# Two decay-matrix buffers, a third gated-output buffer, a later group norm and weight low parts summed by DMA in a Mamba-2 mixer

## The chip, the core and the metric

The kernel runs on one core of a Trainium2 chip. The metric is the device time of one execution in microseconds; the numbers given are the median of the runs and their extremes. A change of 0.3% is about what a measurement of this kernel can tell from none.

## What is computed

One inference step of a two-layer decoder trunk, 576 tokens of width 1024 (512 of a prompt, and 8 sequences of 8 sampled tokens), everything in float32. Layer 0 is a SwiGLU FFN at half weight, a Mamba-2 mixer (SSD) and a second FFN; layer 1 the same with a pooling mixer; then a final norm. Only the SSD is touched. Cut to what matters, it is:

```python
proj = h @ w_in
z, xbc, dt_raw = jnp.split(proj, [D_INNER, D_INNER + CONV_DIM], axis=-1)
xbc, conv_new = causal_dwconv(xbc, conv0, conv_w, conv_b)
xs, Bm, Cm = jnp.split(silu(xbc), ...)          # 32 heads of 64, 8 groups, state 128
dt = softplus(dt_raw + dt_bias);  A = -exp(a_log)
# ssd_scan, in chunks of 128 tokens:
a_cum = cumsum(dt * A)
decay = exp(where(tril, a_cum[l] - a_cum[s], -inf))
y_diag = einsum('bclsgr,bcsgrp->bclgrp', cb[..., None] * decay, x * dt)
y_off  = einsum('bclgn,bclgr,bcgrpn->bclgrp', C, exp(a_cum), h_starts)
y = (y_diag + y_off + d_skip * xs) * silu(z)
y = y * rsqrt(mean over the group's 256 channels of y*y + EPS) * norm_g
return y @ w_out, ssm_new, conv_new
```

## The kernel before

*Matmuls.* Activations lie transposed, channels on the partitions, 576 tokens along the free dimension in two halves of 288. A float32 product is made of three products of rounded parts: weight high by activation high, high by low, low by high. `load` fetches a weight tile of 128 columns (512 KB of the input weight, 256 KB of the output weight) into the pool `raw`, which has two buffers. `block` (L311) makes the parts of up to four 128x128 pieces of it in one `wb` tile, of which the ring has six: ScalarE (ACT) rounds the piece to the high part (L317), and GpSimd (POOL) or VectorE (DVE) subtracts it from the piece for the low part (L318). In the SSD `proj` and `outproj` name POOL for it; the FFNs and the pooling mixer use DVE and POOL as well and stay as they are. `mm` (L334) then issues 24 matmuls for a block of four pieces, 48 for an input projection.

*The SSD.* Of its 48 input projections for z, x, B and C, the two for the first B and C tile take weights that were prepared earlier (`wconv`); 46 go through `proj`. A group loop (L966 to 1003) runs over 8 groups of 4 heads. A group's B and C tiles have been projected and convolved by `conv_in` (L632) during the group before; its two x tiles are projected at its head. `gsum` (L935) squares and sums the two gated outputs of the *previous* group, `rnat` (L184) sums them over the channels on TensorE (PE), and `rstd` (L187 to L198) makes the reciprocal root by two Newton steps on DVE, ten small operations. `gnorm` (L950) lets PE spread the result over all partitions (`rbcast`, L218), multiplies the outputs by it (L955) and splits them into high and low parts `yn`, which `outproj` (L900) multiplies by the output weight in groups 2, 4, 6 and after the loop.

*A pair of heads* (`pair`, L781). The decay matrix `m` (128 x 2 x 576) starts as a broadcast load of the cumulated step sizes `ad` from device memory, issued by SyncE (SP). POOL masks it (L834 to 836), ACT takes the exponential (L839), DVE multiplies it by C times B (L840, L841). Before it is used PE transposes the x tile (L797) and the old states `nat` (L800), DVE copies the latter to `h0t` (L813), and PE multiplies them by C (L822). At the end PE multiplies `m` by the weighted x (L870, L872: the diagonal part `py`). `m` has a single buffer (L787), so that the load for the next pair starts when L872 of this pair is done. The gated output is `yt` (two buffers, L978), the gate `zs` (two buffers, L960).

*The start.* The step sizes go through a chain of small DVE operations (L709 to L745, a softplus by series, a cumulated sum, decay factors), to memory and back, and through transposes on PE (L749 on) into the tables `decp`, `dskp`, `anat`, `wsn` that each pair reads.

*Order.* The engines run their instructions in order. A scheduler puts the written program into one order per engine; the sections `pin` keep some of PE's instructions as written. Two accumulators in PSUM take turns in the SSD: a projection cannot start until DVE has read the one before the last (L638 to 640 for a conv).

Of the kernel before, what the change touches and what calls it, by code (L numbers as in the profile page):

```python
# [8 lines left out]
F32 = mybir.dt.float32  # L9
F32R = mybir.dt.float32r  # L10
I32 = mybir.dt.int32
AF = mybir.ActivationFunctionType
ALU = mybir.AluOpType
# [4 lines left out]
P = 128  # L18
# [3 lines left out]
NB = 8  # L22
NS = 8
T = SEQ + NB * NS
# [25 lines left out]
def trunk(ctx, tc, x_prompt, x_sample, state_ssm, state_conv, state_pool,  # L50
# [26 lines left out]
    def misc():  # L77
        return psum["misc"].tile([P, 512], F32, name="misc")
# [232 lines left out]
    def block(src, eng=None, pool=None):  # L311
        w = (pool or spl).tile([P, 2, 4, P], F32R, name="wb")
        k = src.shape[1]
        hi, lo = w[:, 0, 0:k], w[:, 1, 0:k]
        if src.ndim == 4:
            hi, lo = [a.rearrange("p k (c f) -> p k c f", c=src.shape[2]) for a in (hi, lo)]
        S.copy(out=hi, in_=src)  # L317
        (eng or V).tensor_tensor(out=lo, in0=src, in1=hi.bitcast(F32), op=ALU.subtract)  # L318
        return w

    def load(src, shape):
# [6 lines left out]
    def unit(src, eng=None):  # L328
        kn = src.shape[1]
        v = load(src, src.shape[1:])  # L330
        bl = [block(v[:, k:min(k + 4, kn)], eng) for k in range(0, kn, 4)]
        return [(bl[k // 4][:, 0, k % 4], bl[k // 4][:, 1, k % 4]) for k in range(kn)]

    def mm(pt, w, acts):  # L334
        n, kn = 0, len(acts)
        for (wh, wl), (ah, al) in zip(w, acts):
            for lt, a in ((wh, ah), (wh, al), (wl, ah)):
                for h in range(2):
                    PE.matmul(out=pt[:, h, 0:HALF], lhsT=lt, rhs=a[:, h * HALF:(h + 1) * HALF],  # L339
                              start=n == 0, stop=n == 3 * kn - 1)  # L340
                n += 1
# [246 lines left out]
    def ssd(tail):  # L588
# [5 lines left out]
        with ExitStack() as st:  # L594
# [31 lines left out]

            def proj(c0, w=None):
                pt = acc_tile()
                mm(pt, w or unit(win[:, :, c0:c0 + P], G), hs)
                return pt  # L630

            def conv_in(ct):  # L632
# [111 lines left out]
                ps = slice(32 * r, 32 * r + 32)  # L744
                V.tensor_tensor(out=rhs[ps, :, 4 * r:4 * r + 4], in0=e[ps, P + NS - 1:LW:NS].unsqueeze(1).broadcast_to([32, 16, 4]), in1=bc(mh[ps], 4), op=ALU.mult)  # L745
            V.tensor_scalar(out=mh[0:32], in0=mh[0:32], scalar1=hv[0:32, 2:3], scalar2=None, op0=ALU.mult)
            pt = misc()
            self_ = sel.rearrange("h a b -> h (a b)")
            PE.matmul(out=pt[:, 0:P], lhsT=self_, rhs=rhs.rearrange("h a b -> h (a b)"), start=True, stop=True)  # L749
            PE.matmul(out=pt[:, P:P + 16], lhsT=self_[0:32], rhs=mh[0:32], start=True, stop=True)  # L750
            V.tensor_copy(out=decp, in_=pt[:, 0:P].rearrange("p (a b) -> p a b", b=NB))
            V.tensor_copy(out=dskp, in_=pt[:, P:P + 16])

            pt, pt2 = misc(), misc()
            for i, src in enumerate((ac, q, wd)):
                PE.transpose(out=pt[:, i * P:(i + 1) * P], in_=src[:, 0:P], identity=ident)
                for r in range(2):
                    ps = slice(32 * r, 32 * r + 32)
                    PE.matmul(out=pt2[ps, i * HEADS:(i + 1) * HEADS], lhsT=src[0:64, P:LW], rhs=ident[0:64, ps], start=True, stop=True)
            w3 = dp.tile([64, 3, 32], F32, name="w3")  # L760
            V.tensor_copy(out=w3, in_=wd[0:64, P:LW].unsqueeze(1).broadcast_to([64, 3, 32]))
            for r in range(2):
                ps = slice(32 * r, 32 * r + 32)
                PE.matmul(out=pt2[0:96, P + r * HEADS:P + (r + 1) * HEADS], lhsT=w3.rearrange("h a s -> h (a s)"), rhs=ident[0:64, ps], start=True, stop=True)
            V.tensor_copy(out=wsn, in_=pt2[0:96, P:P + 64].rearrange("s (q h) -> s q h", q=2))
            V.tensor_copy(out=anat[:, 0:4], in_=pt[:, 0:384].rearrange("p (i c h) -> p c i h", i=3, c=4))
            V.tensor_copy(out=anat[0:64, 4], in_=pt2[0:64, 0:96].rearrange("p (i h) -> p i h", i=3))
            V.tensor_scalar(out=anat[:, 0:4, 0], in0=anat[:, 0:4, 0], scalar1=-1.0, scalar2=None, op0=ALU.mult)
            V.tensor_scalar(out=anat[0:64, 4, 0], in0=anat[0:64, 4, 0], scalar1=-1.0, scalar2=None, op0=ALU.mult)

            pin = tc.keep_in_program_order

# [8 lines left out]
            def pair(g, j, bt, ctl, bnat, bblk, cbs, xst, yt):  # L781
# [2 lines left out]
                nat = wk.tile([P, NB, P], F32, name="nat")  # L784
                sv = state_ssm[0, :, h0:h0 + 2].rearrange("b h p n -> (h p) b n")
                nc.sync.dma_start(out=nat, in_=sv)
                m = wk.tile([P, 2, T], F32, name="m", bufs=1)  # L787
                nc.sync.dma_start(out=m, in_=ad[h0:h0 + 2].unsqueeze(0).broadcast_to([P, 2, T]))
                eb = wk.tile([P, T - P], F32, name="eb", bufs=1)
                for h2 in range(2):  # L790
# [109 lines left out]
            def outproj(k0, kn, ds):  # L900
                for d in ds:
                    pd = acc_tile()
                    mm(pd, unit(wout[:, k0:k0 + kn, d * P:(d + 1) * P], G), [yn[k0 + k] for k in range(kn)])
                    add_x(d, pd, 1.0, False)

            def silu(ct, dst):
# [50 lines left out]

            def zproj(k):
                pz = proj(k * P)
                zs = wk.tile([P, T], F32, name="zs")  # L960
                V.tensor_tensor(out=halves(zs), in0=pz[:, :, 0:HALF], in1=rb2, op=ALU.mult)
                S.activation(out=zs, in_=zs, func=AF.Silu)
                return zs

            ys = None
            for g in range(8):  # L966
                bt = gp.tile([P, T], F32, name="bt")
                ctl = gp.tile([P, T], F32, name="ctl")
                silu(16 + g, bt)
                silu(24 + g, ctl)  # L970
                if g == 7:
                    conv_state(2)
                    conv_state(3)
                args = (bt, ctl) + group(bt, ctl)
                xs, nys = [], []

                def run(j):
                    yt = wk.tile([P, T], F32, name="yt")  # L978
                    if g % 2 == 0 and g:
                        outproj(max(2 * g - 6, 0), 4 if g > 2 else 2, range(4 * j, 4 * j + 4))  # L980
                    pair(g, j, *args, xs[j], yt)
                    nys.append(yt)
                    if j == 0 and g < 7:
                        for ct in (17 + g, 25 + g):
                            pre[ct] = conv_in(ct)

                for j in range(2):
                    xst = wk.tile([P, T], F32, name="xst")
                    pre[2 * g + j] = conv_in(2 * g + j)
                    silu(2 * g + j, xst)  # L990
                    if 2 * g + j in (9, 15):
                        conv_state(g // 6)
                    xs.append(xst)
                    if g and j == 0:
                        r = gsum(ys)
                    if g and j == (g < 7):
                        gnorm(g - 1, ys, r)
                    if g == 7:
                        run(j)
                if g < 7:  # L1000
                    run(0)
                    run(1)
                ys = nys
            gtile(7)
# [203 lines left out]
```

## Time and profile before

| | us |
|---|---|
| median of 3 runs | 2381.2 (2376.72 to 2383.12) |
| the profiled execution | 2382.37, its span 2380.6 |
| mean granted clock of PE | 0.978 |

The profile shows one execution, the profiled one, with span times counted from its start. The SSD stage lies from about 417 to 1017 us. In the rows quoted below, a line like `m<-ad` names the tile written and the one read; `x16` is a count of instructions; the granted clock is a share of 2.4 GHz. A wait is put down to the instruction that ended it.

### The profile page before, as it was taken

To read this page: it belongs to the slowest core of one execution; us is meant where nothing else is said; L and a number is where in the kernel's file an instruction comes from. 1 tells how busy PE (TensorE), PEld (TensorE's weight loads), DVE (VectorE), ACT (ScalarE), POOL (GpSimd) and SP (SyncE) were. 2 spreads that over 40 slices of the span, in tenths; PEclk is the share of its full clock that TensorE was granted. 3 is DMA by queue.
4 is the path that set the end of the run, shared out by engine and by line. 5 is a ranking of instruction groups with operands and counts; after the bars stand their busy time and mean duration, and the time that the engine had idled before them with its cause. 6 is when DMAs were issued, how large, how long until landed. Compare 5 with 4: busy or idle time off the path is not lost.

```text
span 2380.6 us, 43792 instructions
## 1 busy us (share of the span) xinstructions
PE 2295.6 (96%) x17572; PEld 2258.1 (95%) x17572; DVE 1888.3 (79%) x2950; ACT 1055.3 (44%) x1949; POOL 1020.2 (43%) x796
## 2 busy tenths in 40 slices
PE   8999999999899899989999999999999999999998
PEld 7999999898899899889999999999999899999997
DVE  8987777678787786799777799788776859778876
ACT  6444435444455445454443355344444344434433
POOL 4555440334334343354545444455531325555530
PEclk9999999999999999999999999999999999999999
DMA  5223222242434334322322322222321242313221
GB/s 148 89 89 107 89 81 65 72 138 83 127 96 121 114 116 127 112 80 72 107 89 89 98 89 81 83 79 88 107 81 58 65 118 89 107 63 98 89 72 58
DMA packets 272903, 222.23 MB, mean 93 GB/s; under 512 B 8321, under 2 KB 269041, under 8 KB 272700
## 3 DMA queue, kind: packets, MB, share of 16 engines
q1 hardware_dynamic: 269172, 218.04, 30.0%
q8 instruction: 139, 2.28, 0.4%
q10 hardware_dynamic: 3528, 1.39, 0.2%
q14 instruction: 64, 0.52, 0.1%
HBM read 206.46 MB, written 12.94 MB: 92 GB/s over the span
## 4 chain that ended last, share of the span: by engine, by line
PE 73%; DVE 17%; DMA 4%; ACT 3%; issue 2%; POOL 0%; SPq 0%; ACTq 0%; DVEq 0%; POOLq 0%
PE acc L370 34%; PE acc L433 21%; PE acc L339 12%; DMA m<-ad 3%; DVE wb L318 3%; DVE cacc L648 2%; DVE wh L256 1%; ACT m L839 1%; PE acc L480 1%; DMA raw<-in_ffn_w_up 1%; DVE ws L1090 1%; PE misc L870 1%; PE misc L826 1%; DVE wh L267 1%; ACT L839 1%
## 5 line engine op out<-in xcount | busy, mean ns | idle before, releaser
L370 PE MATMUL acc<-wh,wb 128*128 128x288 f32 x6888 | 922.1, 295 | 3.2 <-DVE wb L318 1.3
L370 PEld LDWEIGHTS acc<-wh,wb 128*128 128x128 f32 x6888 | 917.6, 189 | 5.0 <-DVE wb L318 2.0
L433 PE MATMUL acc<-ghi,wb 128*128 128x288 f32 x2752 | 482.2, 296 | 0.5 <-DVE x L411 0.5
L317 ACT CAST wb<-raw 128x512 fp32r<-128x512 f32 (+1 forms) x440 | 265.0, 607 | 364.7 <-PE acc L339 155.4
L433 PEld LDWEIGHTS acc<-ghi,wb 128*128 128x128 f32 x2752 | 406.0, 189 | 1.2 <-DVE x L411 1.2
L318 POOL TENSOR_TENSOR wb<-raw,wb 128x512 fp32r<-128x512 f32 (+1 forms) x154 | 207.7, 1351 | 312.1 <-ACT wb L317 294.4
L339 PE MATMUL acc<-hhi,wb 128*128 128x288 f32 x1824 | 336.9, 302 | 0.9 <-DVE m L1065 0.8
L318 DVE TENSOR_TENSOR wb<-ws,wb 128x512 fp32r<-128x512 f32 x328 | 326.6, 1007 | 13.3 <-ACT wb L317 13.2
L318 DVE TENSOR_TENSOR wb<-raw,wb 128x512 fp32r<-128x512 f32 (+1 forms) x286 | 274.4, 975 | 63.5 <-ACT wb L317 63.4
L317 ACT CAST wb<-ws 128x512 fp32r<-128x512 f32 x328 | 202.2, 621 | 233.2 <-PE acc L370 216.8
L433 PE MATMUL acc<-glo,wb 128*128 128x288 f32 x1376 | 294.3, 296 | 0.0
L339 PEld LDWEIGHTS acc<-hhi,wb 128*128 128x128 f32 x1824 | 276.3, 193 | 3.5 <-DVE m L1065 1.1
L411 DVE SCALAR_TENSOR_TENSOR x<-acc,x 128x576 f32<-128x576 f32 x160 | 120.5, 753 | 191.2 <-PE acc L433 190.9
L351 POOL TENSOR_TENSOR ws<-raw,ws 128x512 f32<-128x512 f32 x82 | 154.8, 1887 | 247.9 <-DVE wb L318 241.9
L318 POOL TENSOR_TENSOR wb<-rd,wb 128x512 fp32r<-128x512 f32 x128 | 175.3, 1379 | 183.1 <-ACT wb L317 182.9
L317 ACT CAST wb<-rd 128x512 fp32r<-128x512 f32 x196 | 114.2, 593 | 247.6 <-PE acc L433 212.9
L433 PEld LDWEIGHTS acc<-glo,wb 128*128 128x128 f32 x1376 | 221.4, 189 | 0.0
L339 PE MATMUL acc<-hlo,wb 128*128 128x288 f32 x912 | 201.9, 301 | 0.0
L350 POOL TENSOR_TENSOR ws<-raw 128x512 f32<-128x512 f32 x82 | 123.9, 1511 | 176.3 <-DVE wb L318 176.3
L348 POOL TENSOR_TENSOR ws<-raw 128x512 f32<-128x512 f32 x82 | 125.0, 1525 | 76.7 <-DMA raw<-in_ffn_w_gate 68.9
L339 PEld LDWEIGHTS acc<-hlo,wb 128*128 128x128 f32 x912 | 150.2, 193 | 0.4
L349 POOL TENSOR_TENSOR ws<-ws,raw 128x512 f32<-128x512 f32 x82 | 131.9, 1608 | 8.4 <-DVE wb L318 1.5
(329 smaller groups left out, 2902.8 us busy)
## 6 DMA issues: line engine op xcount, KB each, us to landing
raw<-in_ffn_w_gate SPq DMA_DIRECT2D x41, 1024.0 KB
raw<-in_ffn_w_up SPq DMA_DIRECT2D x41, 1024.0 KB
rd<-in_ffn_w_down SPq DMA_DIRECT2D x80, 512.0 KB
raw<-in_ssd_w_in SPq DMA_DIRECT2D x48, 512.0 KB
m<-ad SPq DMA_DIRECT2D x16, 576.0 KB
nat<-in_state_ssm SPq DMA_DIRECT2D x16, 512.0 KB
out<-nat SPq DMA_DIRECT2D x16, 512.0 KB
raw<-in_ssd_w_out SPq DMA_DIRECT2D x24, 256.0 KB
```

Source lines behind the costliest of these rows:

```text
L317: S.copy(out=hi, in_=src)
L318: (eng or V).tensor_tensor(out=lo, in0=src, in1=hi.bitcast(F32), op=ALU.subtract)
L339: PE.matmul(out=pt[:, h, 0:HALF], lhsT=lt, rhs=a[:, h * HALF:(h + 1) * HALF], start=n == 0, stop=n == 3 * kn - 1)
L348: G.tensor_tensor(out=s[0], in0=blk[2], in1=blk[3], op=ALU.add)
L349: G.tensor_tensor(out=s[1], in0=s[0], in1=blk[0], op=ALU.subtract)
L350: G.tensor_tensor(out=s[2], in0=blk[2], in1=blk[0], op=ALU.subtract)
L351: G.tensor_tensor(out=s[3], in0=blk[1], in1=s[1], op=ALU.subtract)
L370: PE.matmul(out=pt[:, m, 0:HALF], lhsT=wb[:, j, k], rhs=hh[k, h][:, slot], start=n == 0, stop=n == 11)
L411: V.scalar_tensor_tensor(out=halves(x[:, d]), in0=pt[:, :, 0:HALF], scalar=scale, in1=halves(x[:, d]), op0=ALU.mult, op1=ALU.add)
L433: PE.matmul(out=pd[:, q, 0:HALF], lhsT=lt, rhs=a[:, q * HALF:(q + 1) * HALF], start=n == 0, stop=n == 3 * kn - 1)
L648: V.scalar_tensor_tensor(out=a[:, 0:n], in0=ext[:, k:k + n], scalar=cw[:, k * 32 + ct:k * 32 + ct + 1], in1=a[:, 0:n], op0=ALU.mult, op1=A ...
L839: S.activation(out=m[0:n, h2, t0:t0 + n], in_=m[0:n, h2, t0:t0 + n], func=AF.Exp, bias=anat[0:n, c, 0, h0 + h2:h0 + h2 + 1])
```

## The change

It has five parts, all in the SSD.

1. `m` has two buffers (the pool's own number) in place of one.
2. `yt` has three in place of two, `zs` one in place of two.
3. `gnorm` of the previous group is called after the first pair of a group (`run(0)`), where it was called after the projection of the group's second x tile and so ahead of that pair (in the last group after the first x tile).
4. The transposes and copies of the step sizes are put into a function `spread`, called in the first group just ahead of its first pair.
5. In `proj` and `outproj` the low part is not subtracted on POOL: ACT writes the negated high part, and a DMA that POOL issues adds the piece from `raw` to it in place. 124 subtractions of POOL become 124 passes of ACT and 124 such DMAs (116 of 256 KB, 8 of 128 KB); 92 of them belong to the 46 projections, 32 to the output tiles.

```diff
@@ block
         S.copy(out=hi, in_=src)
-        (eng or V).tensor_tensor(out=lo, in0=src, in1=hi.bitcast(F32), op=ALU.subtract)
+        if eng == "dma":
+            S.activation(out=lo, in_=hi.bitcast(F32), func=AF.Identity, scale=-1.0)
+            G.dma_start(out=lo.bitcast(F32), in_=src, accum_op=ALU.add)
+        else:
+            (eng or V).tensor_tensor(out=lo, in0=src, in1=hi.bitcast(F32), op=ALU.subtract)
@@ proj
-                mm(pt, w or unit(win[:, :, c0:c0 + P], G), hs)
+                mm(pt, w or unit(win[:, :, c0:c0 + P], "dma"), hs)
@@ ssd, after the step sizes
-            pt = misc()
-            self_ = sel.rearrange("h a b -> h (a b)")
-            PE.matmul(out=pt[:, 0:P], lhsT=self_, rhs=rhs.rearrange("h a b -> h (a b)"), start=True, stop=True)
...
+            def spread():
+                pt = misc()
+                self_ = sel.rearrange("h a b -> h (a b)")
+                PE.matmul(out=pt[:, 0:P], lhsT=self_, rhs=rhs.rearrange("h a b -> h (a b)"), start=True, stop=True)
...
@@ pair
-                m = wk.tile([P, 2, T], F32, name="m", bufs=1)
+                m = wk.tile([P, 2, T], F32, name="m")
@@ outproj
-                    mm(pd, unit(wout[:, k0:k0 + kn, d * P:(d + 1) * P], G), [yn[k0 + k] for k in range(kn)])
+                    mm(pd, unit(wout[:, k0:k0 + kn, d * P:(d + 1) * P], "dma"), [yn[k0 + k] for k in range(kn)])
@@ zproj
-                zs = wk.tile([P, T], F32, name="zs")
+                zs = wk.tile([P, T], F32, name="zs", bufs=1)
@@ run
-                    yt = wk.tile([P, T], F32, name="yt")
+                    yt = wk.tile([P, T], F32, name="yt", bufs=3)
@@ group loop
                     if g and j == 0:
                         r = gsum(ys)
-                    if g and j == (g < 7):
-                        gnorm(g - 1, ys, r)
                     if g == 7:
                         run(j)
+                        if j == 0:
+                            gnorm(g - 1, ys, r)
                 if g < 7:
+                    if g == 0:
+                        spread()
                     run(0)
+                    if g:
+                        gnorm(g - 1, ys, r)
                     run(1)
                 ys = nys
```

Up to the SSD and after its end the order on PE is the same in both programs. The places that matter are in the SSD; group 5 stands for the others here. The lines of the changed kernel are four or five higher.

PE, before, around the broadcast of the norm of group 4 (`rr`, L218), which is written in group 5 (`acc` is a projection, `s` and `xst` are the first transposes of the pair):

```order
L339 MATMUL acc_9499<-hhi,wb 128x288 x4
L339 MATMUL acc_9499<-hlo,wb 128x288 x2
L218 MATMUL misc<-ident,rr 128x128 x4
L218 MATMUL misc<-ident,rr 128x64
L777 MATMUL misc<-ident,s_9321 96x128 x2
L797 MATMUL misc<-ident,xst 128x128 x4
L797 MATMUL misc<-ident,xst 64x128
```

PE, changed, at the same broadcast:

```order
L866 MATMUL misc<-ident,ht 128x128
L868 MATMUL misc<-ctl,ht 128x128 x3
L870 MATMUL misc<-ident,ch 128x128 x2
L875 MATMUL misc<-m,xdt 64x128 x8
L877 MATMUL misc<-m,xd_4653 64x64 x2
L343 MATMUL acc_9637<-hlo,wb 128x288
L343 MATMUL acc_9637<-hhi,wb 128x288 x4
L343 MATMUL acc_9637<-hlo,wb 128x288 x2
L343 MATMUL acc_9637<-hhi,wb 128x288 x4
L343 MATMUL acc_9637<-hlo,wb 128x288 x2
L343 MATMUL acc_9637<-hhi,wb 128x288 x2
L218 MATMUL misc<-ident,rr 128x128 x4
```

The broadcast stood ahead of the group's first pair; now it stands behind that pair's last matmuls with `m`.

DVE, before, at `rstd` of the same norm (`m` is the matrix of the group's first pair, `rm` the first operation of `rstd`):

```order
L643 COPY tails<-ext 128x24
L840 TENSOR_TENSOR m<-m,cbs 128x2x512
L928 TENSOR_TENSOR bsp<-bns,bsp 32x256
L841 TENSOR_TENSOR m<-m,cbs 64x2x64
L189 TENSOR_SCALAR rm<-misc 128x5
L190 TENSOR_SCALAR rr<-rm 128x5
L192 TENSOR_TENSOR rt<-rr 128x5
L648 SCALAR_TENSOR_TENSOR cacc<-ext,cw,cacc 128x600
```

DVE, changed:

```order
L647 COPY tails<-ext 128x24
L845 TENSOR_TENSOR m<-m,cbs 128x2x512
L846 TENSOR_TENSOR m<-m,cbs 64x2x64
L652 SCALAR_TENSOR_TENSOR cacc<-ext,cw,cacc 128x600 x2
L845 TENSOR_TENSOR m<-m,cbs 128x2x512
L933 TENSOR_TENSOR bsp<-bns,bsp 32x256
L652 SCALAR_TENSOR_TENSOR cacc<-ext,cw,cacc 128x600
L189 TENSOR_SCALAR rm<-misc 128x5
L846 TENSOR_TENSOR m<-m,cbs 64x2x64
```

The multiply of the matrix of the group's second pair has come forward as well: both pairs' L845 now stand ahead of `rstd`, and also ahead of the copies to `h0t` (L818), which follow `rstd`.

POOL, before, in group 5 (the mask of `m`, the subtractions, and `bblk`, which the state update needs):

```order
L834 AFFINE_SELECT m<-m 128x2x512
L835 AFFINE_SELECT m<-m 64x2x64
L836 AFFINE_SELECT m<-m 64x2x64
L318 TENSOR_TENSOR wb<-raw,wb 128x512
L930 TENSOR_TENSOR bblk<-bsp,bmask 96x512 x2
L318 TENSOR_TENSOR wb<-raw,wb 128x512
L636 MEMSET ext 128x3
L318 TENSOR_TENSOR wb<-raw,wb 128x512 x4
```

POOL, changed:

```order
L839 AFFINE_SELECT m<-m 128x2x512
L840 AFFINE_SELECT m<-m 64x2x64
L320 DMA wb<-raw 128x512
L841 AFFINE_SELECT m<-m 64x2x64
L935 TENSOR_TENSOR bblk<-bsp,bmask 96x512 x2
L320 DMA wb<-raw 128x512
L640 MEMSET ext 128x3
L320 DMA wb<-raw 128x512 x2
```

An issue of a DMA now stands where a subtraction stood, also behind the masks that wait for the load of `m`.

## Rows read from the trace of the kernel before

**Rows 1.** Page, part 1: busy time by engine, share of the span, instructions.

```profile
PE 2295.6 (96%) x17572; PEld 2258.1 (95%) x17572; DVE 1888.3 (79%) x2950; ACT 1055.3 (44%) x1949; POOL 1020.2 (43%) x796
```

**Rows 2.** Windows: first FFN, whole SSD stage, and four of its stalls.

```profile
core 0: us, PE busy (x) PEld busy (x) DVE busy (x) ACT busy (x) POOL busy (x), PEclk, DMA share, GB/s
120.00:360.00 240.00, 240.00 (x1811) 240.00 (x1810) 185.49 (x228) 96.11 (x157) 120.13 (x79) 1.00 0.29 91
417.00:1017.00 600.00, 560.63 (x4615) 537.96 (x4615) 462.62 (x1018) 289.48 (x618) 225.93 (x232) 0.96 0.38 111
471.40:486.20 14.80, 9.68 (x49) 8.39 (x49) 8.00 (x20) 5.18 (x11) 4.29 (x5) 0.65 0.32 86
610.40:622.70 12.30, 4.18 (x18) 4.19 (x18) 11.64 (x23) 5.68 (x11) 7.66 (x7) 0.58 0.15 43
817.10:827.50 10.40, 3.74 (x17) 3.24 (x17) 9.05 (x20) 3.80 (x8) 4.58 (x5) 0.67 0.35 98
958.40:964.00 5.60, 3.20 (x15) 2.70 (x15) 4.79 (x15) 3.00 (x6) 1.51 (x2) 0.70 0.21 61
```

**Rows 3.** Waits of PE in the SSD stage: us in total, times, longest.

```profile
PE misc L218 <- DVE rr L197: 20.4, 6, 6.7
PE acc L339 <- DVE ext L640: 8.1, 1, 8.1
PE misc L749 <- DVE rhs L745: 4.7, 1, 4.7
PE acc L339 <- DVE x L409: 2.4, 2, 2.0
PE misc L184 <- DVE sqacc L941: 1.2, 1, 1.2
```

**Rows 4.** Chain of waits, 797 to 826 us (group 5): start us, us, what.

```profile
799.23 0.12 PE misc L872 x4
...
800.51 8.20 DMA m<-ad
...
814.69 1.27 DVE m L841
...
816.07 1.83 DVE rr L190
...
817.93 1.18 DVE rt L192
...
823.77 1.41 PE misc L218 x5
```

**Rows 5.** Chain of waits, 596 to 622 us (group 2).

```profile
598.22 6.76 DMA m<-ad
...
609.27 1.22 DVE m L840
```

**Rows 6.** Chain of waits, 440 to 480 us (start of the SSD).

```profile
450.09 1.25 DVE nat L709
...
460.80 0.25 DVE nat L716
...
462.15 1.25 DVE nat L716
...
468.65 1.31 DVE nat L718
```

**Rows 7.** Instructions of line 648: ns min/median/max, first and last start.

```profile
L648 DVE SCALAR_TENSOR_TENSOR cacc<-ext,cw,cacc x96: 823/844/2646, 439.8 to 973.0; 128x600 f32<-128x600 f32 x96
```

**Rows 8.** Groups by line, SSD stage: busy us, mean ns, idle before and releaser.

```profile
L318 POOL TENSOR_TENSOR wb<-raw,wb 128x512 fp32r<-128x512 f32 (+1 forms) x126 | 171.7, 1365 | 235.7 <-ACT wb L317 218.2 <-ACT tails L642 8.7 <-issue 8.6
...
L317 ACT CAST wb<-raw 128x512 fp32r<-128x512 f32 (+1 forms) x130 | 77.6, 602 | 126.9 <-PE acc L339 116.0 <-DMA raw<-in_ssd_w_out 5.9 <-issue 2.1
```

**Rows 9.** DMA queues, SSD stage: packets, MB, share of 16 engines.

```profile
q1 hardware_dynamic: 104305, 64.28, 37.0%
```

**Rows 10.** Chain of waits, 1005 to 1020 us (256 KB load of an output weight).

```profile
1012.69 4.33 DMA rd<-in_ssd_w_out
```

More of the change, by code (lines that the diff above doesn't have):

```diff
@@ L746, in ssd @@
             V.tensor_scalar(out=mh[0:32], in0=mh[0:32], scalar1=hv[0:32, 2:3], scalar2=None, op0=ALU.mult)
-            pt = misc()
-            self_ = sel.rearrange("h a b -> h (a b)")
-            PE.matmul(out=pt[:, 0:P], lhsT=self_, rhs=rhs.rearrange("h a b -> h (a b)"), start=True, stop=True)
-            PE.matmul(out=pt[:, P:P + 16], lhsT=self_[0:32], rhs=mh[0:32], start=True, stop=True)
-            V.tensor_copy(out=decp, in_=pt[:, 0:P].rearrange("p (a b) -> p a b", b=NB))
-            V.tensor_copy(out=dskp, in_=pt[:, P:P + 16])
@@ L754, in ssd @@
-            pt, pt2 = misc(), misc()
-            for i, src in enumerate((ac, q, wd)):
-                PE.transpose(out=pt[:, i * P:(i + 1) * P], in_=src[:, 0:P], identity=ident)
+            def spread():
+                pt = misc()
+                self_ = sel.rearrange("h a b -> h (a b)")
+                PE.matmul(out=pt[:, 0:P], lhsT=self_, rhs=rhs.rearrange("h a b -> h (a b)"), start=True, stop=True)
+                PE.matmul(out=pt[:, P:P + 16], lhsT=self_[0:32], rhs=mh[0:32], start=True, stop=True)
+                V.tensor_copy(out=decp, in_=pt[:, 0:P].rearrange("p (a b) -> p a b", b=NB))
+                V.tensor_copy(out=dskp, in_=pt[:, P:P + 16])
+                pt, pt2 = misc(), misc()
+                for i, src in enumerate((ac, q, wd)):
+                    PE.transpose(out=pt[:, i * P:(i + 1) * P], in_=src[:, 0:P], identity=ident)
+                    for r in range(2):
+                        ps = slice(32 * r, 32 * r + 32)
+                        PE.matmul(out=pt2[ps, i * HEADS:(i + 1) * HEADS], lhsT=src[0:64, P:LW], rhs=ident[0:64, ps], start=True, stop=True)
+                w3 = dp.tile([64, 3, 32], F32, name="w3")
+                V.tensor_copy(out=w3, in_=wd[0:64, P:LW].unsqueeze(1).broadcast_to([64, 3, 32]))
@@ L757, in ssd @@
                 for r in range(2):
                     ps = slice(32 * r, 32 * r + 32)
[L759 to L769, printed above, removed]
+                    PE.matmul(out=pt2[0:96, P + r * HEADS:P + (r + 1) * HEADS], lhsT=w3.rearrange("h a s -> h (a s)"), rhs=ident[0:64, ps], start=True, stop=True)
@@ new lines, in spread @@
+                V.tensor_copy(out=wsn, in_=pt2[0:96, P:P + 64].rearrange("s (q h) -> s q h", q=2))
+                V.tensor_copy(out=anat[:, 0:4], in_=pt[:, 0:384].rearrange("p (i c h) -> p c i h", i=3, c=4))
+                V.tensor_copy(out=anat[0:64, 4], in_=pt2[0:64, 0:96].rearrange("p (i h) -> p i h", i=3))
+                V.tensor_scalar(out=anat[:, 0:4, 0], in0=anat[:, 0:4, 0], scalar1=-1.0, scalar2=None, op0=ALU.mult)
+                V.tensor_scalar(out=anat[0:64, 4, 0], in0=anat[0:64, 4, 0], scalar1=-1.0, scalar2=None, op0=ALU.mult)
```

## The prediction

> **What bounds the kernel now.** I read the page first. TensorE (PE) is busy for 96% of the span [rows 1], so the time can only come out of the 4% in which it is not, and out of stretches in which its granted clock is low. The table of windows says where they lie: a stretch inside the first FFN has PE busy for all of its 240 us at a clock of 1.00, with 1811 matmuls, that is 0.133 us for one; the SSD stage has it busy for 560.6 of 600 us at a clock of 0.96 [rows 2]. So 39.4 us are idle there. A mean of 0.96 means 0.04 x 600 x 2 = 48 us at the lower of the two levels, 1.2 GHz instead of 2.4, in part while PE was idle anyway: at most 24 us of work lost. The other stages keep their instructions and their order.
>
> The list of PE's waits in the SSD tells what ends the idle time [rows 3]. 20.4 us are six waits of the broadcast of a group's norm factors (L218) for the last step of `rstd` (L197). 8.1 us are one wait for an accumulator that the conv's copy (L640) had not emptied. 4.7 us are the one wait for the step sizes (L745) at the start. PE waits nowhere for a weight's low part (L318); none such is in the list.
>
> The chain of waits shows why `rstd` is late [rows 4]. The diagonal matmuls of one pair end at 799.35 us; only then is the single `m` buffer free. The load that follows lands 8.2 us after 800.51, mask and exponentials follow, and the second multiply of `m` starts on VectorE (DVE) at 814.69, the first some 1.7 us before it. DVE works in order, and `rstd` stands right behind that multiply: 1.83 and 1.18 us for two of its operations, then seven more among other work, and L218 starts at 823.77. PE had reached it 6.66 us before. In the group that waited for L640 it is the same chain: load at 598.22, multiply at 609.27 [rows 5], then `rstd`, then L640.
>
> After a wait PE works at the low level for a while. The window from 817.1 has 0.67: 0.33 x 10.4 x 2 = 6.9 us at half clock, of which PE worked in the last 3.7, so 1.9 us are lost; by the same working the window from 958.4 loses 1.6, the one from 610.4 loses 2.1 and the one from 471.4 loses 4.9 [rows 2].
>
> **The change, part by part.** *Norm broadcast behind the pair.* L218 moves behind the next pair's diagonal matmuls. Counting the instructions in the new order at the durations of the trace, PE now has 26 to 65 us of work between the last use of the buffer and L218, where it had 14 to 20. DVE needs, from that last use, 11.5 us to the first late multiply (10 to 13.6 in the groups read; 11.05 from the load's start in [rows 5], 13.6 in [rows 4]) and 5 to 9.1 us of its own work to the end of `rstd`: 23 us at the worst, under 26. So all six waits go: 20.4 us, and 6 x 1.75 = 10.5 of clock.
>
> *The accumulator wait.* The output projections of that group now come behind the pair as well, and three accumulations lie between the accumulator and its next use. Gone: 8.1 + 2.1 = 10.2.
>
> *Second `m` buffer.* By itself it shortens no work. It lets the first pair of each group have its matrix early. But on DVE the *second* pair's multiply, whose load still starts when the previous pair is finished, stands ahead of `rstd` and of the copies of the first pair's state (`h0t`), for which PE's matmuls at L822 (L827 now) wait. PE's work from the buffer's release to those matmuls is 16 to 47 us, DVE's need 11.5 + 5.3 to 11. In the groups 1 and 2 alone it is short: 17.3 against 17.7 and 16.3 against 16.8; with 13.6 for the 11.5 both wait 2.6 us. I take 2 us for each, nearer the upper end, since the load that I can follow through all its steps [rows 4] is the one of 13.6, and 1.7 of clock: 7.4 given back. The ends are 0 and 8.6.
>
> *Third `yt`, one `zs`.* The third buffer is what lets the norm come a pair later; it costs nothing. `zs` is written by one projection and read by one multiply, before the next pair's projection; nothing, as long as that multiply isn't held for a whole pair (6.4 us of matmuls for a projection, 48 x 0.133).
>
> *Step sizes later.* Some eight matmuls and their copies stand behind more projection work. More important there is the contention: on the chain from 440 us the DVE operations of the softplus take 1.25 to 1.40 us, five times, where another of the same line (L716) takes 0.25 [rows 6]. They run beside the subtractions on GpSimd (POOL), which go. The conv's multiply-add shows the same thing over the stage, 0.82 us at the least and 2.65 at the most [rows 7]. Five times 1.05 is 5.2 us, as much as the 5.1 that PE is idle at this place (14.80 less 9.68 in the window from 471.4 [rows 2]). With the clock's 4.9 there are 10 to be had; I take 7, since ACT becomes busier in the same stretch.
>
> *Smaller waits* (L409, L184; 3.6 us): they are DVE's lateness too; I take 2.
>
> *Low parts by DMA.* Of the window's 126 subtractions of 1.37 us, 172 us together, all but a few leave POOL and in all 124 negations, priced like the cast's 0.60, come to ACT (75 us on 289 of 600) [rows 2, 8]. Neither is the bound. What is new is the landing time L of a 256 KB accumulate, of which the trace has none. From below: the transfers of the stage took 37.0% of 600 us for 64.28 MB [rows 9], so 0.26 MB take 0.9 us, or 1.8 if the destination is read too. From above: the longest landing of `m`, 8.2 us for 576 KB [rows 4]. I take 4.3, that of a 256 KB weight tile [rows 10], the nearest in size.
>
> Two things must hold. A low part must be there before PE wants it: six blocks in the ring give five blocks of 24 matmuls, 16 us, against 0.6 + 0.6 + 1.3 (POOL's issue, bounded by nothing and the subtraction that it replaces) + 4.3 = 6.8; with L = 8.2 it is 10.7. And the two `raw` buffers must turn round in time, since a tile is held until its accumulates have landed. For the 46 projection tiles: load 6.0 (6.76 us for 576 KB in rows 5, scaled to 512), four ACT passes 2.4, issue 1.3, L: 9.7 + L. For the 32 output tiles 4.3 + 1.2 + 1.3 + L = 6.8 + L. The mean is 8.5 + L; two buffers and 78 tiles in 600 us allow 15.4. The stage then takes 78 x (8.5 + L) / 2 us: up to L = 5.8 that is under the 557 of the forecast, at 6.9 it is 600 and all of the gain is gone, and beyond that the kernel is slower. At 4.3 it costs nothing.
>
> Here the Trainium skill speaks against this part. "SBUF — State Buffer", "Who interferes with whom": descriptors of a DMA issued by GpSimd are written through a port that VectorE holds for the whole of an instruction in certain fast modes, copies among them; and "DMA: Bandwidth & Descriptors", "Anatomy of one DMA", gives about 2.0 us plus bytes over 436 GB/s, 2.6 us for this transfer by my estimate. By the second the loop would have 1.7 us more room than I give it; by the first each issue could be held for as long as one DVE instruction. No trace here shows either; the sum stays as it is.
>
> Worked from rows, a hold of an issue by one DVE operation costs up to 1.2 us (the multiply of 609.27 [rows 5]): L = 5.5, still under 5.8, but only just.
>
> **The sum.** 20.4 + 10.5 + 10.2 + 7 + 2 = 50 less 7.4 gives 42.7. The profiled execution took 2382.4 us (1.2 above the median of 2381.2, so the two stand for the same time): **2340 us**. All idle time and 18 us of clock would be 57: 2325; with the whole 24, 2319.
>
> **Rivals.** *1. The waits only move.* The late multiply still stands ahead on DVE; if the load of `m` lands later than now, among the accumulates' traffic (0.38 DMA share [rows 2], some 32 MB more on 64), every group waits at L827, 2 to 4 us plus clock, and the first group loses its 7. For it: the load takes up to 8.2 us already. Against: by the same count PE's margin is 2 to 24 us in the groups 3 to 7. Five more groups at 2 us each are 10 us less gain, at 4.7 and 1.7 of clock 32: 2350 to 2372.
>
> *2. No change.* The turn-round of `raw` takes the place of the norm's waits: an L between 6.7 and 7.1 eats the gain to within 7 us of 2382. For it: ACT's casts and POOL's issues stand in order behind exponentials and masks that wait for `m`. Against: the 4.33 of a tile of this size.
>
> *3. Slower.* The same loop with L over 7.1: with 8.2 the mean tile takes 16.7 us, 78 tiles on two buffers 651, so 51 us more than now, 2433; the sign hangs on 2.8 us of a time that no row shows. For it: an accumulate reads what it writes; and the issue can be held.
>
> Something about 0.3%, 7 us, is what a measurement of this kernel can tell from no change. The forecast, 2325 to 2350, has 0.63; rival 1 0.16; rival 2 0.08; rival 3 0.13. So faster 0.79, the same 0.08, slower 0.13. The range takes in the forecast, rival 1 and the edge of rival 2, with the 2319 of the fullest gain at its lower end: 2320 to 2376.
>
> **What would show it.** Right: L218 gone from PE's list of waits, the SSD's stretch of 600 us some 43 shorter at a clock of 0.98 or more, the conv's multiply-add near 0.84 us at its longest, waits of 2 us at L827 in two early groups, no wait of PE on a weight block. Wrong: a wait of PE at L343 on a DMA into `wb`, waits of SP's queue for `raw` that end with an accumulate, landings of over 6 us for it, or waits at L827 in all groups.

## The result and the profile after

The changed kernel takes 2404.85 us (median of 4 runs, 2401.27 to 2407.57) where the kernel before takes 2381.39 in the same runs: the ratio is 1.0101, with an interval of 1.0079 to 1.0122. It is slower by 1%; the forecast was 2340. The profiled execution has a span of 2405.8 us, 25.2 more than before.

The window of the whole SSD stage, from the first transposes of the convolution's state to the last output tile, shows where the time went. The first row below is the kernel before, the second the changed one (columns as in [rows 2]).

```profile
428.50:1015.70 587.20, 547.83 (x4506) 525.55 (x4505) 457.60 (x998) 286.82 (x614) 221.96 (x221) 0.96 0.39 111
```

```profile
428.40:1041.40 613.00, 558.19 (x4505) 533.06 (x4504) 401.68 (x1000) 355.28 (x741) 165.00 (x221) 0.95 0.68 159
```

The stage is 25.8 us longer, all of the difference. PE's idle time in it rose from 39.4 (587.20 less 547.83) to 54.8 us; the time at the lower clock rose from 47.8 to 58.0 us, of which PE worked in 37.8 and 51.3, so that it costs 6.7 us more. That leaves 3.7 us of the 25.8, in PE's busy time, which no row explains. DVE is busy for 56 us less, although it runs as many instructions (998 and 1000), POOL for 57 less, ACT for 68 more, and the DMA engines are busy for 0.68 of the stage where it was 0.39. The page has a queue that was not there before, and the landing time that no row of before could show:

```profile
q0 software_dynamic: 17856, 31.47, 7.8%
...
wb<-raw POOLq DMA_DIRECT2D x116, 256.0 KB, 4.0
```

An accumulate of 256 KB lands 4.0 us after its issue, in the median; the forecast had taken 4.3. Its 31.47 MB take 7.8% of sixteen engines' span, 5.96 us of one such share per MB (0.078 x 2405.8 / 31.47), where the 218 MB of the loads and stores take 3.3.

PE's waits in the stage (us in total, times, longest) answer to [rows 3]:

```profile
PE acc L343 <- DVE x L413: 10.6, 6, 3.6
PE misc L782 <- ACT s L780: 6.3, 1, 6.3
PE misc L827 <- ACT h0t L815: 6.2, 3, 3.6
PE misc L866 <- DVE ht L861: 5.6, 2, 3.4
PE misc L805 <- DVE rm L189: 4.7, 2, 3.3
PE misc L782 <- ACT fin L890: 4.4, 2, 2.2
```

The wait at L218 is gone altogether, and of the 8.1 for the conv's copy 3.8 are left. In their place PE waits in other places for ACT and DVE. The first row had 2.4 us before (L409 in [rows 3]) and the fourth 1.0; the other four were not in the list. None is a wait for a weight block. SP's waits from 417 to 1040 us tell what is behind them, first of the changed kernel, then of the one before:

```profile
SPq L329 <- DMA wb<-raw: 381.9, 74, 16.0
```

```profile
SPq L325 <- POOL wb L318: 287.6, 59, 12.8
```

SP stands for 382 us at the next weight load, waiting for an accumulate to land. Before, SP's wait cost PE nothing, as the weight was there when ACT wanted it; now ACT waits for it. Of ACT's waits, the first row is its wait for a free weight block, that is for PE (116.0 before [rows 8]); the others are for raw tiles, 93 us together, where the kernel before has 5.9 for output tiles [rows 8] and 1.1 for projection tiles (last row):

```profile
ACT wb L317 <- PE acc L343: 63.9, 37, 4.1
ACT wb L317 <- DMA raw<-in_ssd_w_out: 53.2, 18, 6.5
ACT wb L317 <- DMA raw<-in_ssd_w_in: 39.9, 15, 6.6
```

```profile
ACT wb L317 <- DMA raw<-in_ssd_w_in: 1.1, 1, 1.1
```

ACT works in order, so a cast that waits for its raw tile also holds the copies behind it that PE wants. Of PE's four waits of 2 us or more for ACT's `h0t` and `fin`, three come right behind such a cast (at 513, 723 and 873 us), the fourth behind the exponentials of `m`.

The chain of waits from 554 us shows how this reaches `m` (start us, us, what):

```profile
558.94 2.29 DMA raw<-in_ssd_w_out
...
561.25 0.04 POOLq L320
...
562.59 5.20 DMA wb<-raw
...
567.85 0.37 SPq L329
...
568.33 4.29 DMA m<-ad
...
572.69 1.28 ACT L844
```

An accumulate lands; only then can SP issue the next load of a raw tile; and the load of `m` stands behind that on SP's queue. The buffer of this `m` had been free since 563.1, when the last matmuls with the matrix that was in it had ended. Over the pairs 2 to 15 the load of `m` is issued more than 1 us after its buffer is free in eight, by 1.1 to 5.4 us, and from issue to mask it takes 7.4 us in the mean, where it took 6.2 before.

### The profile page after: what moved, and what is told of

Its sections match the earlier page's. It is cut to its first block, busy times and chain, and to the rows that moved or that the text cites. A ratio compares the mean times of both kernels' runs of the same rounds, so it can differ in the third digit from the quotient of the medians.

```text
span 2405.8 us, 44158 instructions
## 1 busy us (share of the span) xinstructions
PE 2304.3 (96%) x17572; PEld 2264.2 (94%) x17572; DVE 1822.1 (76%) x2950; ACT 1122.6 (47%) x2075; POOL 958.6 (40%) x796
## 3 DMA queue, kind: packets, MB, share of 16 engines
q0 software_dynamic: 17856, 31.47, 7.8%
q10 hardware_dynamic: 3528, 1.39, 0.2%
## 4 chain that ended last, share of the span: by engine, by line
PE 68%; DVE 14%; DMA 9%; issue 4%; ACT 4%; POOL 1%; SPq 0%; POOLq 0%; DVEq 0%; ACTq 0%
PE acc L374 34%; PE acc L437 21%; PE acc L343 9%; DMA wb<-raw 3%; DVE wb L322 3%; DMA m<-ad 3%; DVE wh L256 1%; DMA raw<-in_ssd_w_in 1%; DMA raw<-in_ssd_w_out 1%; ACT m L844 1%; PE acc L484 1%; ACT wb L317 1%; DVE cacc L652 1%; DVE ws L1099 1%; DVE wh L267 1%
## 5 line engine op out<-in xcount | busy, mean ns | idle before, releaser
L322 DVE TENSOR_TENSOR wb<-raw,wb 128x512 fp32r<-128x512 f32 (+1 forms) x286 | 265.3, 942 | 72.5 <-ACT wb L317 72.3
L320 POOL DMA_DIRECT2D wb<-raw x124 | 107.7, 875 | 319.9 <-ACT wb L319 202.2
```

The costliest lines, as they stand in the source:

```text
L320: G.dma_start(out=lo.bitcast(F32), in_=src, accum_op=ALU.add)
```

## The experiments

The SSD of every kernel here is put in order anew by the scheduler, so each edit moves more than the part it names. Two edits that remove nothing PE waited for at length (e12, and m on ACT's queue in e14) cost 7 to 9 us. A difference of that size between two kernels, e1's gain of 9 us among them, is therefore no proof of a cause by itself; where one is named below, a row of waits shows it. Ratios are to the kernel before on the same chip.

| kernel | what it is | us | ratio (interval) |
|---|---|---|---|
| after | the change | 2404.85 | 1.0101 (1.0079 to 1.0122) |
| e1 | change without the DMA part | 2373.42 | 0.997 (0.9954 to 0.9987) |
| e2 | DMA part alone | 2425.41 | 1.0182 (1.0165 to 1.0199) |
| e3 | change, 3 raw, 4 wb | 2382.86 | 1.0001 (0.9991 to 1.0011) |
| e4 | change, 4 wb | 2401.27 | 1.0086 (1.0063 to 1.011) |
| e5 | change, raw in 4 halves | 2390.58 | 1.0039 (1.0024 to 1.0054) |
| e6 | e5 without DMA part | 2371.65 | 0.9964 (0.995 to 0.9977) |
| e7 | change, m on ACT's queue | 2401.6 | 1.0082 (1.0065 to 1.0099) |
| e8 | change, DMA for output tiles alone | 2381.23 | 1.0005 (0.9995 to 1.0014) |
| e9 | e5 and m on ACT's queue | 2354.98 | 0.9879 (0.9852 to 0.9906) |
| e10 | e5, negation on DVE | 2379.93 | 0.9992 (0.9978 to 1.0007) |
| e11 | e1 with the early norm | 2382.06 | 0.9996 (0.9986 to 1.0006) |
| e12 | e1, `tails` copied by ACT | 2382.67 | 0.9999 (0.9987 to 1.0011) |
| e13 | e9 without DMA part | 2380.04 | 0.9994 (0.9984 to 1.0004) |
| e14 | e1 and m on ACT's queue | 2379.99 | 0.999 (0.9979 to 1.0002) |

**e1: the reordering alone.** Against the changed kernel:

```diff
-                mm(pt, w or unit(win[:, :, c0:c0 + P], "dma"), hs)
+                mm(pt, w or unit(win[:, :, c0:c0 + P], G), hs)
...
-                    mm(pd, unit(wout[:, k0:k0 + kn, d * P:(d + 1) * P], "dma"), [yn[k0 + k] for k in range(kn)])
+                    mm(pd, unit(wout[:, k0:k0 + kn, d * P:(d + 1) * P], G), [yn[k0 + k] for k in range(kn)])
```

> The change without its fifth part: the low parts in the SSD are subtracted on POOL as before, the other four parts stay. Theory A (the two raw buffers, now held until an accumulate has landed, pace the SSD): 2340 us (2325 to 2355), as the forecast's sum without the DMA part; L218 gone from PE's waits, SP's waits for raw end with a subtraction again. Rival B (the new order is what costs: norm behind the pair, both multiplies of m ahead of rstd): 2390 us or more, with PE's waits at L782, L805 and L827 as in the changed kernel. Rival C (m's load stands behind raw loads on SP's queue and lands later in the accumulates' traffic): like A here, 2340 to 2355.

It takes 2373.42 us: faster than before by 0.3%, and 31 under the changed kernel. So the DMA part is what made the change slower, and rival B falls; but theory A's 2340 falls with it, since the rest gains 9 us, not 40. PE's waits of e1 (417 to 1007 us) show why:

```profile
PE acc L343 <- DVE x L413: 8.5, 6, 3.3
PE misc L754 <- DVE rhs L749: 3.9, 1, 3.9
PE misc L827 <- DVE h0t L818: 3.4, 4, 1.5
PE acc L343 <- DVE ext L644: 2.9, 1, 2.9
PE misc L866 <- DVE ht L861: 2.7, 1, 2.7
PE misc L802 <- DVE rm L189: 2.4, 1, 2.4
```

L218 is gone as forecast. The waits that stand here are for DVE in other places. In the chain from 562 us DVE works off the norm (L960), the split (L409) and the copies of the next pair (L814) one after the other while PE waits for the conv's copy (L642 to L644) to free its accumulator:

```profile
562.54 1.70 DVE yt L960 x4
...
564.80 0.76 DVE yn L409
...
566.22 1.56 DVE yn L409
567.79 0.60 DVE xw L814
...
569.51 0.36 DVE ext L642
...
570.45 1.62 PE acc L343 x7
```

The norm put behind the first pair falls into the stretch in which DVE has to close one pair and open the next. And DVE is slow beside POOL's products and subtractions, which read two tiles each: one copy of 128x24 took 3.45 us while POOL ran its two `bblk` products and two subtractions (first row DVE, the others POOL):

```profile
721.70 3.45 DVE L647 COPY tails<-ext 128x24 f32<-128x24 f32 x1
```

```profile
719.65 3.02 POOL L935 TENSOR_TENSOR bblk<-bsp,bmask 96x512 fp32r<-96x512 f32 x2 [2.02 <-DVE bsp L933]
722.64 2.48 POOL L322 TENSOR_TENSOR wb<-raw,wb 128x512 fp32r<-128x512 f32 x2
```

**e2: the DMA part alone**, the same two calls and the branch in `block` put into the kernel before.

```diff
+        if eng == "dma":
+            S.activation(out=lo, in_=hi.bitcast(F32), func=AF.Identity, scale=-1.0)
+            G.dma_start(out=lo.bitcast(F32), in_=src, accum_op=ALU.add)
```

> The kernel before with the fifth part alone: low parts by negation and accumulating DMA. Theory A: 2400 to 2440 us, slower than the kernel before by 20 or more, since the raw loop now takes 15.3 us a tile (mean of the changed kernel's 74 full cycles) and the norm's waits are all still there. Rival B: 2375 to 2390, the DMA part alone changes nothing. Rival C: 2390 to 2410, the late m makes each of the six norm waits 2 to 4 us longer.

2425.41 us, 1.8% slower than before and inside theory A's bounds: the DMA part costs 43 us on the old order, 31 on the new one. One reason that theory A gave did not hold, however. The norm's waits are not all still there; of the six and 20.4 us two are left:

```profile
PE misc L218 <- DVE rr L197: 8.4, 2, 8.1
```

**e3 and e4: three raw buffers.**

```diff
-    raw = ctx.enter_context(tc.tile_pool(name="raw", bufs=2))
-    spl = ctx.enter_context(tc.tile_pool(name="spl", bufs=6))
+    raw = ctx.enter_context(tc.tile_pool(name="raw", bufs=3))
+    spl = ctx.enter_context(tc.tile_pool(name="spl", bufs=4))
```

> The changed kernel with three raw buffers; to make room the ring of weight blocks (wb) has four instead of six, which the FFNs use too. To be held against e4, which has the four alone. Theory A: 40 us or more under e4, PE's idle time in the SSD under 25 us, SP's wait for an accumulate under 150 us. Rival B: within 10 us of e4. Rival C: 15 to 30 us under e4, since raw loads wait less ahead of m on SP.

> The changed kernel with four weight blocks (wb) in the ring instead of six, nothing else: the control of e3. All theories: 2405 to 2450 us; the ring gives 3 blocks of 24 matmuls, 9.6 us, of lead where it gave 16, so that a late low part reaches PE sooner. Under theory A it is at the slow end, 2420 or more, as the accumulate's path takes 6.8 us of the 9.6; under B and C 2405 to 2420.

e4, with four weight blocks, is 2401.27, no slower than the change with six and under the 2405 that all theories had as their least: the lead of a low part over PE is not what binds. e3 is 18 us under it, and ACT's waits for raw tiles have all but gone, from 93 us in the change to 5:

```profile
ACT wb L317 <- DMA raw<-in_ssd_w_out: 2.6, 1, 2.6
ACT wb L317 <- DMA raw<-in_ssd_w_in: 2.5, 1, 2.5
```

The third buffer gives back somewhat over half of what the DMA part costs, within the bounds of rival C and short of theory A's 40; SP still waits 342 us for accumulates, more than theory A's 150. The ring is part of the cause, not all.

**e5 and e6: the same memory in four halves.** An SSD tile fills half a raw buffer or a quarter of it. Cut in four, the pool gives the SSD four buffers; an FFN tile is loaded as two.

```diff
-    raw = ctx.enter_context(tc.tile_pool(name="raw", bufs=2))
+    raw = ctx.enter_context(tc.tile_pool(name="raw", bufs=4))
...
-        rw = raw.tile([P, 2048], F32, name="raw")
+        rw = raw.tile([P, 1024], F32, name="raw")
...
-            return prep(fp, [load(w[:, :, p * 256:(p + 1) * 256], (8, 256)) for w in (wg, wu)], n)
+            return prep(fp, [[load(w[:, 4 * q:4 * q + 4, p * 256:(p + 1) * 256], (4, 256)) for q in range(2)] for w in (wg, wu)], n)
```

> The changed kernel with the same memory of the pool raw cut into four tiles of half the size: an SSD tile (which filled half a raw buffer or a quarter) now has four buffers to turn in, an FFN tile is loaded in two halves. Theory A (turn-round of raw): the DMA's cost goes, 2350 us (2340 to 2365), SP's wait for an accumulate under 150 us where it was 382. Theory D (the new order gained only 9 us in e1 because POOL's subtractions hold DVE, as in the copy of 3.45 us beside them) adds that it is under e1's 2373 by 10 or more. Rival C (m late by SP's queue or by the traffic of accumulates): traffic stays, 2380 to 2395. Rival E (issues held on POOL behind the masks of m): 2385 to 2400.

> As e5, but with the low parts subtracted on POOL: the control that tells what the halves do by themselves, in the FFNs and to e1. All theories: within 8 us of e1, 2366 to 2381, since neither kernel waits for raw on PE. A result over 2385 would say that loading the FFN's tiles in halves costs, and e5 would have to be read against it.

e6 is at 2371.65, so the halves do nothing by themselves. e5 is at 2390.58, within the bounds of rivals C and E and far over theory A's: 14 us of the 31 are back, 19 are not. ACT's list in e5 has no wait for an SSD raw tile any more, so the ring is no longer what it waits for. SP still waits 315 us for accumulates, which tells little, as SP loads each tile as soon as its buffer is free and so waits in every kernel. What holds `m` now is another load on SP's queue (start us, us, line, what):

```profile
705.58 0.63 SPq L853 DMA_DIRECT2D out<-nat  x1
712.82 0.37 SPq L792 DMA_DIRECT2D nat<-in_state_ssm  x1
713.29 0.72 SPq L329 DMA_DIRECT2D raw<-in_ssd_w_in  x1
714.11 3.56 SPq L794 DMA_DIRECT2D m<-ad  x1
```

The load of `nat` waits until the store out of its buffer, issued at 705.6, has landed; behind it the load of `m` goes out at 714.1, although its buffer had been free since 708.2. SP waits 65.3 us for such stores in e5; in e1 it is 27.5.

**e7 and e9: m on ACT's queue**, on the change and on e5.

```diff
-                nc.sync.dma_start(out=m, in_=ad[h0:h0 + 2].unsqueeze(0).broadcast_to([P, 2, T]))
+                nc.scalar.dma_start(out=m, in_=ad[h0:h0 + 2].unsqueeze(0).broadcast_to([P, 2, T]))
```

> The changed kernel with the load of m issued by ACT's queue instead of SP's, so that it no longer stands behind raw loads that wait for accumulates. Theory A: within 8 us of the changed kernel, 2397 to 2412. Rival C: 2375 to 2390, 15 us or more faster, and the waits of PE that go back to a late m (L782 for ACT's copy behind the exponentials, L805 for rstd) gone.

> e5 (accumulating DMA, four half raw tiles) with the load of m issued by ACT. In e5 the load of m is issued 6 to 7 us after its buffer is free in five of 14 pairs, behind a load of nat that waits on SP's queue for the store out of the same buffer. Theory C (this lateness is the rest of the DMA's cost, 19 us of e5 over e6): 2370 to 2380, and the free-to-issue time under 1 us. Theory F (the rest is ACT's: 124 more passes of 0.61 us stand among m's exponentials and the copies PE waits for): within 6 us of e5, 2384 to 2397, since ACT gets 16 issues more.

On the change (e7) the time stays the same within the intervals, 3 us less, as theory A had it. But e7 does not put `m` right: its load is still issued more than 1 us late in five of 14 pairs, by 2.0 to 5.6 us, since ACT's queue is in order too and ACT still waits 96 us for raw tiles:

```profile
ACT wb L317 <- DMA raw<-in_ssd_w_in: 53.3, 22, 8.9
ACT wb L317 <- DMA raw<-in_ssd_w_out: 42.5, 11, 7.6
```

What an early `m` is worth while raw tiles are late, e7 thus leaves open. On e5 the same edit (e9) gives 36 us, well over the 11 to 21 that theory C allowed: e9 takes 2354.98 us and is the fastest kernel of the study, 1.2% under the kernel before. Its load of `m` is issued within 0.1 us of the release in all pairs, and the window of its whole SSD has 21.1 us of idle time:

```profile
425.90:987.60 561.70, 540.58 (x4505) 518.71 (x4504) 404.06 (x1000) 349.25 (x737) 167.59 (x221) 0.98 0.74 173
```

That the DMA engines are at 0.74 there, more than in the changed kernel, says that their traffic by itself was not what cost the time.

**e8: DMA for the 32 output tiles alone**, `proj` with POOL's subtraction as in e1.

> The changed kernel with accumulating DMA for the 32 output tiles alone (one block each), the 46 projection tiles subtracted on POOL. Theory A: 2368 to 2382, close to e1: a cycle of an output tile takes 11.1 us, under the 15.4 that two buffers allow, so these tiles leave the loop its slack. Rival E: 2380 to 2395, since also these issues stand behind the masks of m.

2381.23, 8 us over e1: it lies in both bounds and tells the theories not apart. The output tiles did not leave the ring all its slack, though: ACT waits 42 us for raw tiles, none in e1.

**e10: negation on DVE**, in e5.

```diff
-            S.activation(out=lo, in_=hi.bitcast(F32), func=AF.Identity, scale=-1.0)
+            V.tensor_scalar(out=lo, in0=hi.bitcast(F32), scalar1=-1.0, scalar2=None, op0=ALU.mult)
```

> e5 with the negation of the high part on DVE (tensor_scalar by -1) in place of ACT. Theory F: 2370 to 2380, PE's waits at L783 for ACT's copies (9.5 us in e5) gone. Theory C: 2384 to 2397. Rival G (the low part's path is then through a DVE that is behind in its own queue, and POOL's issues wait for it): 2395 or more.

2379.93, 11 us under e5 and just within theory F's bounds: it points at a cost of ACT's 124 passes, which the forecast had put at nothing. The waits for ACT's copies at L783, 9.5 us in e5, are down to 2.8. The 11 us are what is left after DVE has taken the passes, and not far over what a new order alone can move. It was not tried together with e9's queue.

**e11: the norm where it was**, in e1.

```diff
                     if g and j == 0:
                         r = gsum(ys)
+                    if g and j == (g < 7):
+                        gnorm(g - 1, ys, r)
                     if g == 7:
                         run(j)
-                        if j == 0:
-                            gnorm(g - 1, ys, r)
...
                     run(0)
-                    if g:
-                        gnorm(g - 1, ys, r)
                     run(1)
```

> e1 (no DMA part) with the norm where it was before, ahead of the group's first pair: two m buffers, the later step sizes and the yt and zs numbers stay. Theory H (the late norm is what gains, as the late multiply of m still stands ahead of rstd on DVE): 2378 to 2386, the waits at L218 back with 15 us or more. Rival I (the second m buffer is what gains, and the late norm only puts DVE work between the two pairs, as in e1's chain where DVE runs norm, split, xw and xdt while PE waits): 2360 to 2372, faster than or equal to e1, L218's waits under 8 us.

2382.06, the time of the kernel before, with this row among PE's waits:

```profile
PE misc L218 <- DVE rr L197: 15.4, 6, 5.3
```

So the second `m` buffer without the late norm gains nothing, as theory H had it: the multiply of the later `m` stands ahead of `rstd`, as the order had shown. It is the late norm that takes PE past it; the row shows this, not the 9 us between e1 and e11.

**e12: the copy to `tails` on ACT**, in e1 (`V.tensor_copy` for the samples' part becomes `S.copy`).

> e1 with the conv's copy to tails (128x24, L647) on ACT in place of DVE. In e1 this copy took up to 3.45 us beside POOL's bblk and subtractions, 0.17 in the median. Theory D (POOL's reads hold DVE): 2364 to 2371, 3 to 9 us under e1. Rival: the hold falls on the next DVE instruction, within 3 us of e1, 2370 to 2377.

2382.67, 9 us slower than e1: both expectations missed. The copies take 0.22 us at most on ACT, but the scheduler's new order puts other waits in (L866 for DVE 6.5 us, 2.7 in e1). So e12 tells nothing about the hold, either way.

**e13 and e14: m on ACT's queue without the DMA part.**

> e9 (four half raw tiles, m loaded by ACT's queue) with the low parts subtracted on POOL again. Theory J (the accumulating DMA by itself gains once raw and SP's queue no longer hold things, because POOL's reads no longer hold DVE): 2365 to 2375, 10 us or more over e9's 2355. Theory K (the DMA part is at best neutral, and e9 gains by m's load alone): 2340 to 2358.

> e1 (no DMA part, two raw buffers) with the load of m issued by ACT. In e1 that load is issued within 0.1 us of its buffer's release in all pairs but two, so SP's queue does not hold it. Both theories of e13: within 6 us of e1, 2367 to 2380. A result of 2360 or less would say that ACT's queue helps m in another way than by SP's waits.

Both take 2380 us, 7 to 8 more than the same kernels with `m` on SP (e14 against e1, at the edge of what was allowed; e13 against e6). So m on ACT's queue gains nothing by itself, and e9 is 25 us under e13 by the DMA part alone: theory J, with e13 even above its bounds. The same part that cost 31 us between e1 and the change gains 25 here. The conv's multiply-add shows what it gains by (busy us, mean ns; in order: before, after, e9, e13):

```profile
L648 DVE SCALAR_TENSOR_TENSOR cacc<-ext,cw,cacc 128x600 f32<-128x600 f32 x96 | 101.3, 1055 | 11.5 <-ACT cacc L646 10.6
```

```profile
L652 DVE SCALAR_TENSOR_TENSOR cacc<-ext,cw,cacc 128x600 f32<-128x600 f32 x96 | 83.8, 872 | 54.3 <-ACT cacc L650 53.4
```

```profile
L653 DVE SCALAR_TENSOR_TENSOR cacc<-ext,cw,cacc 128x600 f32<-128x600 f32 x96 | 84.0, 875 | 36.0 <-ACT cacc L651 35.1
```

```profile
L653 DVE SCALAR_TENSOR_TENSOR cacc<-ext,cw,cacc 128x600 f32<-128x600 f32 x96 | 96.9, 1010 | 20.0 <-ACT cacc L651 19.1
```

With subtractions on POOL it takes 1.01 to 1.06 us in the mean, without them 0.87. Within the kernel before, the 45 of them that ran beside a product or subtraction of POOL took 1.30 us in the mean and the 51 others 0.84; in e13 it is 1.24 and 0.85. So it is POOL's work beside it that makes DVE slow.

## Why the prediction was wrong

**The step that failed** is the turn-round of the raw buffers: "At 4.3 it costs nothing." The landing time under it was right, 4.0 measured; the loop built around it was too short, by the waits of queues that were known. From load to load of the same buffer the forecast's sum gives 8.5 + 4.0 = 12.5 us for the mean tile, of 15.4 allowed. The trace has 15.3 over 74 cycles of the changed kernel (all but the first two, which wait for the SSD to begin): 5.8 from the load's issue to the first cast (forecast 5.3), 5.1 from there to the last accumulate's issue (1.9 of ACT's passes in the forecast), 0.9 for the issue (1.3), 3.5 to the next load's issue. What is missing, some 3 us, is in the second of these. ACT's other work between the passes is 1.8 us of it (0.7 for the exponentials of `m`), and ACT's waits there 0.9; and 8 of the 124 issues stood 1.3 to 7.0 us on POOL behind a mask of `m`. The forecast named these queues under rival 2 and gave them no time. The mean cycle proves nothing by itself: SP loads a tile as soon as its buffer is free (within 0.6 us in 74 of 76 cycles), so that the cycle follows the length of the stage, and the kernel before has 14.8 by the same count. That the ring came to hold the kernel up is shown by ACT's waits for raw tiles, 7 us before and 93 after, and by e3 and e5, in which they are 5 and 0 and of the DMA part's cost 18 and 14 us are back.

**A step that was left out** is what stands behind a raw load on SP. The forecast had the load of `m` start when its buffer is free. With accumulates holding the raw loads, and stores holding those of `nat`, it starts up to 5.4 us later, 7.0 in e5. The chain above and e9 show this. With the ring and this queue both relieved (e9) the DMA part gains 25 us where it cost 31, so these two outweigh whatever else it costs.

**The negations** were put at nothing, as ACT is not the bound. e10 puts them at up to 11 us in e5, where they stand among `m`'s exponentials and the copies that PE waits for; this rests on one pair of kernels, and a new order alone moves nearly as much.

**The terms of the sum.** The six norm waits, 20.4 us, went as forecast, and of the 8.1 us of the accumulator 2.9 are left in e1 and 3.8 in the change. But the 36 us of e1's share of the forecast (42.7 less the 7 at the start, which need POOL's subtractions gone) came to 9: the waits moved. Rival 1 named that, at another place: not L827, which has 3.4 us in e1, but the accumulators and transposes that wait for DVE while it works off the late norm between two pairs. The start, too: in e1 the wait for the step sizes is 3.9 us against 4.7; in the changed kernel it is no longer in the list, and the longest operation of L720 (L716 before) takes 0.35 us where it took 1.39. That bears the term out as far as the wait goes.

**What the rivals said.** Rival 3 had the right loop and the right sign, with a chance of 0.13, but it hung the sign on L over 7.1, and the loss came with 4.0. The bound had been put on the one unknown number, and the known queues were left out of the loop. Of the signs that the forecast gave of being wrong, PE's wait on a DMA into `wb` and waits at L827 in all groups did not come, landings over 6 us came in 13 of 124, and SP's waits that end with an accumulate came in full. That last one would have come with a gain as well: e9 has 284 us of them.

The rule of the Trainium skill ("SBUF — State Buffer", "Who interferes with whom") that VectorE can hold the writing of descriptors hardly shows in the time of the issues: the median of the 124 is 0.87 us, the longest 1.32, and three are over 1.0. Whether it is in their landings, which range from 2.7 to 9.1 us, no run here tells. The estimate after the Trainium skill ("DMA: Bandwidth & Descriptors", "Anatomy of one DMA"), 2.6 us, is under the 4.0 measured in a stretch with other traffic; the measurement decides.

Not settled is why the scheduler's orders of near-equal programs (e1, e12, e14) differ by 7 to 9 us, and how much of e10's 11 us is of that kind.

## What to carry to other kernels

When an instruction is replaced by a DMA, the buffer that it reads is held until the landing: add up the whole cycle of that buffer with the waits of every in-order queue in it, casts, issues and loads, and see what else stands on the queue that waits for it. That a ring was not waited for before the change says nothing about after; here cutting its tiles in half and taking one critical load off the waiting queue turned a loss of 1.0% into a gain of 1.2%. And where an in-order engine has its bursts, as DVE between two pairs, moving a step past one wait can put it into the next.

## What the runs showed of the hardware

An accumulate from one place in on-chip memory to another landed 4.0 us after its issue (256 KB, median of 116) and took 1.8 times the engine time per MB of the kernel's loads and stores (5.96 against 3.3 us). POOL was held 0.88 us by the issue of one. A DVE copy of 128x24, 0.17 us in the median of e1, took 3.45 us once beside POOL's products and subtractions, and the multiply-add of 128x600 took 1.30 us in the mean beside them and 0.84 away from them (the kernel before).
